# A decoder layer on one Trainium2 core: the third norm's sum of squares, one weight block's remainder, the first loads and the final norm's root, each placed otherwise

## The chip, the cores and the metric

The kernel runs on one core of a Trainium2 chip. The metric is the device time of one execution in microseconds (us). The core has a matmul engine (TensorE, PE), three engines for elementwise work (VectorE or DVE, ScalarE or ACT, GpSimd or POOL), a queue for transfers (SyncE, SP), and sixteen DMA engines. Each engine works through its own list of instructions in order; semaphores hold an instruction until what it needs is there.

## The reference, cut to what matters

One layer for 256 tokens of width 1024, in float32:

```python
h = rmsnorm(x, norm_mix_g)
proj = h @ w_in                               # q, k, v, gu, gv, two gates
y_a = moba_attention(rope(q), rope(k), v) @ moba_w_proj
y_b = gmlp_spatial_gating(gu, gv, ...) @ gmlp_w_proj
x = x + (sigmoid(gate_a) * y_a + sigmoid(gate_b) * y_b) @ w_out
x = x + cross_attention(rmsnorm(x, norm_xa_g), rmsnorm(mem, norm_mem_g), ...)
h = rmsnorm(x, norm_ffn_g)                    # the third norm
q = h @ peer_w_q                              # 8 heads, 2 halves of 128
s1, i1 = top_k(q[half 0] @ subkeys[0].T, 16); s2, i2 = top_k(q[half 1] @ subkeys[1].T, 16)
e, g = best 16 of the sums s1 + s2, softmax   # 16 of 128*128 experts for each head
x = x + sum over e of g * gelu(h . w_down[e]) * w_up[e]
return rmsnorm(x, final_g)
# rmsnorm(x, g) = x * rsqrt(mean(x*x) + 1e-6) * g
```

The last sum is computed densely: all 16384 experts are multiplied, 128 blocks of the down product and 128 blocks of the up product, with weights that are zero for the experts not chosen.

## The kernel before

**Number format.** PE gets each float32 matrix as two parts, a rounded one and the remainder. A weight block (128 x 1024, 512 KB) is loaded into a tile `raw` by SP's queue, ACT casts it to `hi` (L140), and another engine subtracts, `lw = raw - hi` (L142). A product then takes three matmuls: hi by hi, lo by hi, hi by lo (L179 to L181 in `mm3`). Activations are split in the same way by `split` (L170, L173, L175).

**Order.** The order of work is written out by hand. `stream` lists the weight blocks: 84 of the front part (`f`), then those of the down (`d`) and up (`u`) products. `take(kind)` hands out the next block, and at the same time issues the cast and remainder of the block two further on (`conv_to`, LEAD = 2) and loads up to four further still (`load_to`, four `raw` tiles), and then the postponed pieces in `later`. So when block m is used, block m+2 is being converted.

**Who makes the remainder.** `lo_engine` chooses: VectorE for front blocks below 70, POOL from 70 on and for the first five `d` blocks, VectorE after that. Blocks in the list `spread` (52 to 59, 65 to 69) have their remainder put off: two half-width subtractions on VectorE go into the list `half`, and `half.pop(0)()` at a later place in the code issues one of them (L146).

**Cross-attention.** For head h, `xquery(h)` computes queries, `xscore(h)` the scores, their row maximum (L629, L630) and the exponentials on ACT (L632); `xscale(h)` divides by the sum (L652, L654); `xtrans` transposes (L641) and copies (L644, L646). Two `nm_.step()` calls (blocks 62 and 63) finish the values `vm` from the memory, which are scaled at L688 and L689; `xvalue` (L661) multiplies. The first `nm_.step()` stands ahead of `xscore(3)`, and it converts block 64, whole, before the change.

**Third norm.** `Squares.add` squares one of eight pieces of x on ACT (L261) and adds it to a running sum on VectorE (L267), so there are seven adds. `Squares.matmul` sums over partitions on PE (L273). The 16 blocks 68 to 83 of `peer_w_q` run in a loop over n; each calls `take`, multiplies (`tblock`), copies the result on ACT, and runs `pscore(n-1)`: two score matmuls (L752), a copy on ACT (L753) and a top-16 pass on VectorE (`best`, L728 to L736). The products use unnormalised activations; the root `r3` (`newton`: ACT's root and five small VectorE instructions) is needed only for the later normalised activations `h3`, which `norm_block(k)` makes one piece at a time. `bcast` spreads the root over the partitions by a matmul (L286). Before the change the squares are added for pieces 0 to 2, 3 to 5, and 6 and 7 at n = 0, 1, 2; the sum's matmul stands in the middle of block n = 3; the broadcast stands at n = 7, and the eight norm blocks at n = 7 to 14.

**After the loop.** VectorE selects the 16 best pairs of each head and looks up their indices, in pieces between which the first 22 `down` blocks are placed.

**End.** `ulast` runs the last two up blocks for token half t = 0, then t = 1. For each t, ACT squares both halves of the row (L1082), with their sums; VectorE adds these and forms the mean (L1084, L197), ACT takes the root (L1086), VectorE multiplies by the gain (L1087), refines the root and scales (L1095; POOL for t = 0), and the result is stored.

Of the kernel before, what the change touches and what calls it, by code (L numbers as in the profile page):

```python
# [16 lines left out]
F32 = mybir.dt.float32  # L17
# [4 lines left out]
AF = mybir.ActivationFunctionType  # L22
OP = mybir.AluOpType
# [3 lines left out]
D = 1024  # L27
S = 256
KD = 8
EPS = 1e-6  # L30
# [15 lines left out]
N_XO, N_PQ = 4, 16  # L46
# [43 lines left out]
def body(tc, I, out, dbg=None):  # L90
# [3 lines left out]
    V, A, P, T, SY = nc.vector, nc.scalar, nc.gpsimd, nc.tensor, nc.sync  # L94
# [10 lines left out]
    nf = I["wf"].shape[0]  # L105
    steps = plan()
    stream = [("f", n) for n in range(nf)] + [x for x in steps if x[0] in "du"]
    raws, convs, later = {}, {}, []
    spread, half = [*range(52, 60), nf - N_PQ - 3, *range(nf - N_PQ - 2, nf - N_PQ + 2)], []
    pos = {"load": 0, "conv": 0, "take": 0}  # L110

    def load_to(n):
        while pos["load"] < min(n, len(stream)):
            m = pos["load"]
            kind, idx = stream[m]
            raw = wst.tile([128, 1024], F32, name="raw", bufs=RAW)
            SY.dma_start(raw, {"f": I["wf"], "d": I["wd"], "u": I["wu"]}[kind][idx])
            raws[m] = raw
            pos["load"] += 1

    def lo_engine(m):
        kind, idx = stream[m]
        if kind == "f":
            return V if idx < nf - N_PQ + 2 else P
        if kind == "d" and idx < FIRST:
            return P
        return V
# [23 lines left out]
    def take(kind):  # L151
        m = pos["take"]
        assert stream[m][0] == kind
        pos["take"] += 1
        conv_to(m + 1 + LEAD)
        load_to(m + 1 + LEAD + RAW)
        for fn in later:
            fn()
        later.clear()
        return convs.pop(m)  # L160


    def sl(k):
        return (slice(None), k, slice(None))

    def tsl(t):
        return slice(t * 128, (t + 1) * 128)

    def split(hi, lo, src, scale=1.0, eng=None):
        A.activation(hi, src, AF.Copy, scale=scale)  # L170
        e = eng or V
        if isinstance(scale, float) and scale == 1.0:
            e.tensor_sub(lo, src, hi.bitcast(F32))  # L173
        else:
            e.scalar_tensor_tensor(lo, src, scale, hi.bitcast(F32), op0=OP.mult, op1=OP.subtract)  # L175

    def mm3(ps, w, wsl, x, xsl, start, stop):
        (wh, wl), (xh, xl) = w, x
        T.matmul(ps, wh[wsl], xh[xsl], start=start, stop=False)  # L179
        T.matmul(ps, wh[wsl], xl[xsl], start=False, stop=False)  # L180
        T.matmul(ps, wl[wsl], xh[xsl], start=False, stop=stop)  # L181
# [14 lines left out]
    def mean_sq(v, ms, width):  # L196
        V.tensor_scalar(v, ms, 1.0 / width, EPS, op0=OP.mult, op1=OP.add)  # L197
# [5 lines left out]
    mid = ctx.enter_context(tc.tile_pool(name="mid", bufs=1))  # L203
# [4 lines left out]
    def pair(name, pool, n=KD, w=S):  # L208
        return (pool.tile([128, n, w], F32R, name=name + "h"), pool.tile([128, n, w], F32R, name=name + "l"))
# [4 lines left out]
    def pmm():  # L214
        return pf.tile([128, S], F32, name="mm", bufs=3)

    def pat(shape):
        return pf.tile(shape, F32, name="at", bufs=3)
# [4 lines left out]
    xT = fo.tile([128, KD, S], F32, name="xT")  # L223
# [5 lines left out]
    raw0 = wst.tile([128, 1024], F32, name="raw", bufs=RAW)  # L229
    raws[0] = raw0  # L230
    pos["load"] = 1
    for k in range(2):
        SY.dma_start(raw0[:, k * 512:(k + 1) * 512], I["wf"][0][:, k * 512:(k + 1) * 512])
        SY.dma_start(xT[:, k], I["xT"][:, k])
    for j in range(1, 4):
        SY.dma_start(xT[:, 2 * j:2 * j + 2], I["xT"][:, 2 * j:2 * j + 2])
        load_to(j + 1)
    warm = cst.tile([128, 1], F32, name="warm")
    A.activation(warm, ones, AF.Sqrt)
    wps = pat([128, 128])  # L240
# [48 lines left out]
    def tblock(w, x, n=KD, base=0, mid=None):  # L289
        ps = pmm()  # L290
        for k in range(n):
            if mid and k == n // 2:
                mid()
            c = (base + k) * 128
            mm3(ps, w, (slice(None), slice(c, c + 128)), x, sl(k), k == 0, k == n - 1)
        return ps
# [23 lines left out]
    raw0 = raws.pop(0)  # L320
# [57 lines left out]
    for c in range(4):  # L378
        for nm in ("q", "k"):
            first = c == 0  # L380
            ps = tblock(take("f"), xg, mid=(sqp.matmul if nm == "q" else rope_norm) if first else None)
# [139 lines left out]
    for c in range(4):  # L521
        ps = tblock(take("f"), xg)
# [37 lines left out]
    for c in range(4):  # L560
        ps = tblock(take("f"), mg)
# [42 lines left out]
    pq = Squares(fp2, "x1")  # L604
    for c in range(KD):
        ps = tblock(take("f"), mp)
# [30 lines left out]
    def xtrans(t, h):  # L637
        ps = pat([128, 2, 2, 128])
        for i in range(2):
            for sb in range(2):  # L640
                T.transpose(ps[:, i, sb], Px[t][:, h + i, sb * 128:(sb + 1) * 128], ident)  # L641
        PT = fp2.tile([128, 2, 2, 128], F32, name="PT", bufs=4)
        if t:
            V.tensor_copy(PT, ps)  # L644
        else:
            A.copy(PT, ps)  # L646
        XT_[t, h] = PT


    def xscale(h):  # L650
        xr = fp2.tile([128, 2], F32, name="xr", bufs=4)
        V.reciprocal(xr, xs[:, :, 2, h])  # L652
        for t in range(2):
            V.tensor_scalar(Px[t][:, h], Px[t][:, h], xr[:, t:t + 1], None, op0=OP.mult)  # L654
# [26 lines left out]
    xscale(2)  # L681
    xtrans(0, 0)
    xtrans(1, 0)
    skh = [fo.tile([128, 8, 128], F32, name="kT")]
    P.dma_start(skh[0], I["skT"][:, 0:8])
    xscale(3)
    nm_.step()
    V.tensor_scalar(vm[:, 0], nm_.ps[0], rm[:, 0:1], None, op0=OP.mult)  # L688
    A.activation(vm[:, 1], nm_.ps[1], AF.Copy, scale=rm[:, 1:2])  # L689
# [8 lines left out]
    xg2 = pair("xg", fo)  # L698
    rp = rs1.enter_context(tc.tile_pool(name="route", bufs=2, side="right", reuse_waits="tile"))
    S1 = rp.tile([128, 8, 2, 2, 128], F32, name="S1", bufs=1)  # L700
    x2T = rp.tile([128, KD, S], F32, name="x2T", bufs=1)
    pq = Squares(fp2, "x2")
    for c2 in range(4):
        w = take("f")
        for c in range(2):
            cc = 2 * c2 + c
            ps = tblock(w, oxT, n=4, base=4 * c)
# [32 lines left out]
    def norm_block(k):  # L740
        hx = fp2.tile([128, S], F32, name="hx", bufs=3)
        V.scalar_tensor_tensor(hx, x2T[:, k], gcol[:, 3, k:k + 1], r3bc, op0=OP.mult, op1=OP.mult)
        later.append(lambda: split(h3[0][:, k], h3[1][:, k], hx))
# [12 lines left out]
    for n in range(16):  # L756
        sk = skh[n // 8][:, n % 8]
        w = take("f")
        if n == 4:
            v3 = fp2.tile([128, 2], F32, name="v3")  # L760
            sq_sum(pq, v3)
        if n == 5:
            r3 = newton(fp2, v3, 2, "r3")
            V.tensor_copy(r3c, r3)
        ps = tblock(w, xg2, mid=pq.matmul if n == 3 else None)
        qp = fp2.tile([128, S], F32, name="qp", bufs=2)
        A.copy(qp, ps)
        qps[n] = (qp, sk)
        if n < 3:
            for k in range(3 * n, min(3 * n + 3, 8)):  # L770
                pq.add(x2T[:, k], A, V)
        if n == 7:
            bcast(r3, r3bc)
            norm_block(0)
        if 8 <= n < 15:
            norm_block(n - 7)
        if n > 0:
            pscore(n - 1)
    pscore(15)
# [6 lines left out]
    gp = g.enter_context(tc.tile_pool(name="exp", bufs=2, reuse_waits="tile"))  # L786
    pp = g.enter_context(tc.tile_pool(name="pexp", bufs=1, space=PSUM, reuse_waits="tile"))
    yps = [[pp.tile([128, 512], F32, name=f"y{t}{z}") for z in range(2)] for t in range(2)]
# [89 lines left out]
    n, spent = 0, 0.0  # L878
# [39 lines left out]
    for j in range(3):  # L918
        ps = mblock()[:, :S]
# [112 lines left out]
    for n, x in enumerate(rest):  # L1032
# [16 lines left out]
        else:  # L1049
            up_a(x[1])  # L1050
            up_b(x[1])
            w = take("u")
# [18 lines left out]
    sqs = wst.tile([128, D], F32, name="raw", bufs=RAW)  # L1071
    for t in range(2):
        ulast(ws, [UP[i2] for i2 in range(128 - TAILN, 128)], t)
        scale = P.tensor_scalar if t == 0 else V.tensor_scalar
        fs = gp.tile([128, 2], F32, name="fs")
        yg = wst.tile([128, D], F32, name="raw", bufs=RAW)
        fm = gp.tile([128, 1], F32, name="fm")
        fv = gp.tile([128, 1], F32, name="fv")
        sq = gp.tile([128, 1], F32, name="fsq")
        for z in range(2):  # L1080
            zs = slice(z * 512, (z + 1) * 512)
            A.activation(sqs[:, zs], yps[t][z], AF.Square, accum_out=fs[:, z:z + 1])  # L1082
            if z == 1:
                V.tensor_add(fm, fs[:, 0:1], fs[:, 1:2])  # L1084
                mean_sq(fv, fm, D)
                A.activation(sq, fv, AF.Sqrt)  # L1086
            V.tensor_mul(yg[:, zs], yps[t][z], fg[:, zs])  # L1087
        fy = gp.tile([128, 1], F32, name="fy")
        V.reciprocal(fy, sq)
        fu = gp.tile([128, 1], F32, name="fu")  # L1090
        V.scalar_tensor_tensor(fu, fy, fy, fv, op0=OP.mult, op1=OP.mult)
        V.tensor_scalar(fu, fu, -0.5, 1.5, op0=OP.mult, op1=OP.add)
        for z in range(2):
            zs = slice(z * 512, (z + 1) * 512)
            scale(yg[:, zs], yg[:, zs], fy, fu, op0=OP.mult, op1=OP.mult)  # L1095
            (SY if z == 0 or t == 0 else A).dma_start(out[0, tsl(t), zs], yg[:, zs])
    g.close()
    ctx.close()

# [73 lines left out]
```

## Time and profile before

| | |
|---|---|
| median of three runs | 1051.2 us |
| lowest, highest | 1049.24, 1052.67 us |
| the profiled execution | 1049.31 us, of which the span shown is 1047.6 us |
| PE busy | 1029.6 us, 98% of the span |
| VectorE busy | 763.3 us, 73% |
| ACT busy | 593.9 us, 57% |
| POOL busy | 63.5 us, 6% |
| mean granted clock of PE | 0.996 of full speed |

The lines of the timeline have the start and the duration in us, the engine, the source line, the operation, the tile written and the tiles read, the shape and a count. In brackets stands for how long the engine was idle before it, and what ended that. The lines of a window have busy us and the number of instructions for PE, PE's weight loads, DVE, ACT and POOL, then PE's granted clock, the share of the DMA engines and GB/s. Lines of the waits have the total in us, how often, and the longest.

### The profile page before, as it was taken

Reading aid. Unit: us, or ns where it says so; the run is one execution under the profiler, and the core shown is the slowest. Engines: PE = TensorE matmul, PEld = TensorE weight load, DVE = VectorE, ACT = ScalarE, POOL = GpSimd, SP = SyncE. Lnnn points to the kernel's source line nnn. Section 1 sums busy time; section 2 is a strip of 40 time slices with the busy share of each in tenths; the row PEclk is TensorE's granted clock in tenths of the full one; section 3 lists DMA queues with packets and bytes.
Section 4 is the critical chain, followed back from the end, with each engine's and each line's share of the span. In section 5 each row is a group of like instructions: output and inputs, shape, how many; then the busy total and the mean of one; then the engine's idle time right before and its main releaser. Section 6 shows DMA issues by size and latency. Waiting matters only on the chain.

```text
span 1047.6 us, 19742 instructions
## 1 busy us (share of the span) xinstructions
PE 1029.6 (98%) x7862; PEld 953.1 (91%) x7862; DVE 763.3 (73%) x1502; ACT 593.9 (57%) x935; POOL 63.5 (6%) x53
## 2 busy tenths in 40 slices
PE   9999999998999999999999999999999999999997
PEld 7989999998999999999988998899999988888885
DVE  6765797688999899965656565666799766666666
ACT  6955745665654567755454545454678654444554
POOL 0400000016740000000000000000000000000000
PEclk9999999999999999999999999999999999999999
DMA  8644655554456534456666566656444565656562
GB/s 291 232 138 133 197 173 168 174 164 140 157 165 203 171 118 155 147 180 189 194 188 194 185 198 187 195 185 198 149 157 140 181 192 191 196 188 197 187 198 101
DMA packets 52365, 185.84 MB, mean 177 GB/s; under 512 B 5937, under 2 KB 6833, under 8 KB 52145
## 3 DMA queue, kind: packets, MB, share of 16 engines
q1 hardware_dynamic: 51552, 183.20, 54.6%
q8 instruction: 61, 1.00, 0.4%
q0 software_dynamic: 288, 1.05, 0.3%
q10 hardware_dynamic: 432, 0.34, 0.1%
q14 instruction: 32, 0.25, 0.1%
HBM read 183.52 MB, written 1.05 MB: 176 GB/s over the span
## 4 chain that ended last, share of the span: by engine, by line
PE 89%; DVE 7%; ACT 2%; DMA 1%; issue 1%; DVEq 0%; SPq 0%; ACTq 0%
PE A L179 11%; PE y L1016 11%; PE y L1013 11%; PE y L1012 11%; PE A L181 11%; PE A L180 11%; PE mm L179 5%; PE mm L180 5%; PE mm L181 5%; PE m L985 2%; PE m L984 2%; DVE lw L142 1%; ACT hi L140 1%; DMA raw<-in_wf 1%; PE at L406 1%; PE nat L312 1%
## 5 line engine op out<-in xcount | busy, mean ns | idle before, releaser
L142 DVE TENSOR_TENSOR lw<-raw,hi 128x1024 fp32r<-128x1024 f32 (+1 forms) x309 | 377.1, 1222 | 229.9 <-ACT hi L140 229.0
L140 ACT CAST hi<-raw 128x1024 fp32r<-128x1024 f32 (+1 forms) x341 | 355.4, 1043 | 189.4 <-issue 139.5
L179 PE MATMUL A<-mgh,hi 128*128 128x256 f32 x1024 | 290.2, 283 | 0.0
L181 PE MATMUL A<-mgh,lw 128*128 128x256 f32 x1024 | 287.6, 281 | 1.8 <-DVE lw L142 1.8
L180 PE MATMUL A<-mgl,hi 128*128 128x256 f32 x1024 | 287.4, 281 | 0.0
L181 PEld LDWEIGHTS A<-mgh,lw 128*128 128x128 f32 x1024 | 195.8, 191 | 2.2 <-DVE lw L142 2.2
L1012 PE MATMUL y<-hi,gahl 128*128 128x512 f32 x504 | 196.1, 389 | 0.0
L1013 PE MATMUL y<-lw,gahl 128*128 128x512 f32 x504 | 196.1, 389 | 0.0
L180 PEld LDWEIGHTS A<-mgl,hi 128*128 128x128 f32 x1024 | 192.8, 188 | 2.2
L179 PEld LDWEIGHTS A<-mgh,hi 128*128 128x128 f32 x1024 | 192.3, 188 | 2.2
L1016 PE MATMUL y<-hi,gahl 128*128 128x512 f32 x504 | 155.2, 389 | 0.0
L800 ACT ACTIVATE aring<-A 128x256 f32<-128x256 f32 x128 | 49.2, 384 | 161.7 <-PE A L181 161.7
L179 PE MATMUL mm<-xgh,hi 128*128 128x256 f32 x416 | 119.1, 286 | 0.3 <-DVE q L368 0.3
L181 PE MATMUL mm<-xgh,lw 128*128 128x256 f32 x416 | 116.4, 280 | 0.0
L180 PE MATMUL mm<-xgl,hi 128*128 128x256 f32 x416 | 116.4, 280 | 0.0
L1016 PEld LDWEIGHTS y<-hi,gahl 128*128 128x128 f32 x504 | 94.6, 188 | 19.6
L1012 PEld LDWEIGHTS y<-hi,gahl 128*128 128x128 f32 x504 | 94.6, 188 | 17.4
L1013 PEld LDWEIGHTS y<-lw,gahl 128*128 128x128 f32 x504 | 94.6, 188 | 17.4
L179 PEld LDWEIGHTS mm<-xgh,hi 128*128 128x128 f32 x416 | 79.0, 190 | 1.3 <-issue 0.7
L181 PEld LDWEIGHTS mm<-xgh,lw 128*128 128x128 f32 x416 | 79.1, 190 | 0.0
L180 PEld LDWEIGHTS mm<-xgl,hi 128*128 128x128 f32 x416 | 78.9, 190 | 0.1
L986 ACT ACTIVATE G<-m 128x512 f32<-128x512 f32 x64 | 66.0, 1141 | 5.0 <-PE m L985 2.3
(272 smaller groups left out, 1246.8 us busy)
## 6 DMA issues: line engine op xcount, KB each, us to landing
raw<-in_wd SPq DMA_DIRECT2D x128, 512.0 KB, 3.8
raw<-in_wu SPq DMA_DIRECT2D x128, 512.0 KB, 4.1
raw<-in_wf SPq DMA_DIRECT2D x83, 512.0 KB, 3.7
memT<-in_memT SPq DMA_DIRECT2D x1, 1024.0 KB, 7.3
xT<-in_xT SPq DMA_DIRECT2D x3, 256.0 KB, 6.7
out_y<-raw SPq DMA_DIRECT2D x3, 256.0 KB, 2.0
raw<-in_wf SPq DMA_DIRECT2D x2, 256.0 KB, 3.5
wmT<-in_wsT SPq DMA_DIRECT2D x1, 512.0 KB, 6.2
```

The costliest lines, as they stand in the source:

```text
L140: A.copy(hi[:, ps], raw[:, ps])
L142: lo_engine(m).tensor_sub(lw[:, ps], raw[:, ps], hi[:, ps].bitcast(F32))
L179: T.matmul(ps, wh[wsl], xh[xsl], start=start, stop=False)
L180: T.matmul(ps, wh[wsl], xl[xsl], start=False, stop=False)
L181: T.matmul(ps, wl[wsl], xh[xsl], start=False, stop=stop)
L800: A.activation(a, ps, AF.Gelu_apprx_tanh)
L984: T.matmul(ps[:, t], a1[at], bh[at], start=True, stop=False)
L985: T.matmul(ps[:, t], a1[at], bl[at], start=False, stop=True)
L986: A.activation(Gq[q][:, :, s * TG + c:s * TG + c + 8].rearrange("p i t -> p t i"), ps, AF.Copy, scale=1.0 / 16384.0)
L1012: T.matmul(yps[t][z], gh[:, tsl(t)], wh[:, zs], start=False, stop=False, skip_group_check=True)
L1013: T.matmul(yps[t][z], gh[:, tsl(t)], wl[:, zs], start=False, stop=False, skip_group_check=True)
L1016: T.matmul(yps[t][z], gl[:, tsl(t)], wh[:, zs], start=False, stop=False, skip_group_check=True)
```

## The change

Four edits:

1. Third norm. The remainders of blocks 70 and 71 move from POOL to VectorE. The squares go 4, 3, 1 over n = 0, 1, 2. The sum's matmul moves from the middle of block n = 3 to its end, behind ACT's copy of the result in the order of the code and ahead of `pscore(2)`. The root's broadcast and the norm blocks move one block earlier, to n = 6 and n = 6 to 13.
2. Cross-attention. The remainder of block 64 is put off in two halves; one is issued behind the first two transposes, the other behind `xscale(3)`.
3. First loads. `xT` comes in three transfers (two, two and four of its eight pieces) instead of five (one, one, two, two, two), ordered with the first weight blocks as the diff shows.
4. Final norm. ACT squares with a scale of 1/32, so that its sums are already means; eps is added to the first half's sum while the second is still being computed, and ACT takes the root of the second sum with that as its bias. For t = 1 the two small factors are multiplied first, and the row is scaled half by ACT and half by VectorE.

```diff
-    spread, half = [*range(52, 60), nf - N_PQ - 3, *range(nf - N_PQ - 2, nf - N_PQ + 2)], []
+    spread, half = [*range(52, 60), nf - N_PQ - 4, nf - N_PQ - 3, *range(nf - N_PQ - 2, nf - N_PQ + 2)], []
...
-            return V if idx < nf - N_PQ + 2 else P
+            return V if idx < nf - N_PQ + 4 else P
...
-    for k in range(2):
-        SY.dma_start(raw0[:, k * 512:(k + 1) * 512], I["wf"][0][:, k * 512:(k + 1) * 512])
-        SY.dma_start(xT[:, k], I["xT"][:, k])
-    for j in range(1, 4):
-        SY.dma_start(xT[:, 2 * j:2 * j + 2], I["xT"][:, 2 * j:2 * j + 2])
-        load_to(j + 1)
+    SY.dma_start(raw0[:, 0:512], I["wf"][0][:, 0:512])
+    SY.dma_start(xT[:, 0:2], I["xT"][:, 0:2])
+    SY.dma_start(raw0[:, 512:1024], I["wf"][0][:, 512:1024])
+    SY.dma_start(xT[:, 2:4], I["xT"][:, 2:4])
+    load_to(2)
+    SY.dma_start(xT[:, 4:8], I["xT"][:, 4:8])
+    load_to(4)
...
     xtrans(1, 0)
+    half.pop(0)()
...
     xscale(3)
+    half.pop(0)()
     nm_.step()
...
-        ps = tblock(w, xg2, mid=pq.matmul if n == 3 else None)
+        ps = tblock(w, xg2)
...
-        if n < 3:
-            for k in range(3 * n, min(3 * n + 3, 8)):
-                pq.add(x2T[:, k], A, V)
-        if n == 7:
+        for k in ((0, 1, 2, 3), (4, 5, 6), (7,))[n] if n < 3 else ():
+            pq.add(x2T[:, k], A, V)
+        if n == 3:
+            pq.matmul()
+        if n == 6:
             bcast(r3, r3bc)
-            norm_block(0)
-        if 8 <= n < 15:
-            norm_block(n - 7)
+        if 6 <= n < 14:
+            norm_block(n - 6)
...
-            A.activation(sqs[:, zs], yps[t][z], AF.Square, accum_out=fs[:, z:z + 1])
-            if z == 1:
-                V.tensor_add(fm, fs[:, 0:1], fs[:, 1:2])
-                mean_sq(fv, fm, D)
-                A.activation(sq, fv, AF.Sqrt)
+            A.activation(sqs[:, zs], yps[t][z], AF.Square, scale=1.0 / 32.0, accum_out=fs[:, z:z + 1])
+            if z == 0:
+                V.tensor_scalar(f0, fs[:, 0:1], EPS, None, op0=OP.add)
+            else:
+                A.activation(sq, fs[:, 1:2], AF.Sqrt, bias=f0)
             V.tensor_mul(yg[:, zs], yps[t][z], fg[:, zs])
+        V.tensor_scalar(fv, fs[:, 1:2], f0, None, op0=OP.add)
...
-        for z in range(2):
-            zs = slice(z * 512, (z + 1) * 512)
-            scale(yg[:, zs], yg[:, zs], fy, fu, op0=OP.mult, op1=OP.mult)
-            (SY if z == 0 or t == 0 else A).dma_start(out[0, tsl(t), zs], yg[:, zs])
+        if t == 0:
+            for z in range(2):
+                zs = slice(z * 512, (z + 1) * 512)
+                P.tensor_scalar(yg[:, zs], yg[:, zs], fy, fu, op0=OP.mult, op1=OP.mult)
+                SY.dma_start(out[0, tsl(t), zs], yg[:, zs])
+        else:
+            fr = gp.tile([128, 1], F32, name="fr")
+            V.tensor_scalar(fr, fu, fy, None, op0=OP.mult)
+            A.activation(yg[:, 0:512], yg[:, 0:512], AF.Copy, scale=fr)
+            V.tensor_scalar(yg[:, 512:], yg[:, 512:], fr, None, op0=OP.mult)
+            SY.dma_start(out[0, tsl(t), 512:], yg[:, 512:])
+            A.dma_start(out[0, tsl(t), 0:512], yg[:, 0:512])
```

More of the change, by code (lines that the diff above doesn't have):

```diff
@@ L1073, in body @@
         ulast(ws, [UP[i2] for i2 in range(128 - TAILN, 128)], t)
-        scale = P.tensor_scalar if t == 0 else V.tensor_scalar
         fs = gp.tile([128, 2], F32, name="fs")
         yg = wst.tile([128, D], F32, name="raw", bufs=RAW)
-        fm = gp.tile([128, 1], F32, name="fm")
+        f0 = gp.tile([128, 1], F32, name="fm")
         fv = gp.tile([128, 1], F32, name="fv")
```

## The prediction, made before the change was timed

> **What bounds the kernel now.** I read the page first, then what TensorE (PE) waited for, then the timeline around each of its waits.
>
> ```profile
> span 1047.6 us, 19742 instructions
> PE 1029.6 (98%) x7862; PEld 953.1 (91%) x7862; DVE 763.3 (73%) x1502; ACT 593.9 (57%) x935; POOL 63.5 (6%) x53
> ```
>
> PE is busy in all but 18 us. So an edit pays only where it takes away a PE wait, a stretch in which PE runs slowly, or time at either end of the span. The longest waits of PE, in the columns total, times, longest:
>
> ```profile
> PE at L273 <- DVE sq L267: 4.2, 1, 4.2
> PE A L181 <- DVE lw L142: 1.8, 2, 1.4
> PE nat L312 <- ACT hi L140: 1.2, 1, 1.2
> ```
>
> The first is the third norm's and the third the start's, both touched here. The change also works on a gap in cross-attention and on the final norm, which lies behind PE's last matmul.
>
> **Third norm.** PE around its wait (start, duration in us), and a window with its granted clock (the column PEclk, third from the end):
>
> ```profile
> 238.53 0.61 PE L752 MATMUL at<-kT,qp 128*128 128x128 f32 x4
> 238.89 0.36 PE L179 MATMUL mm<-xgh,hi 128*128 128x256 f32 x1
> ...
> 240.27 0.28 PE L181 MATMUL mm<-xgh,lw 128*128 128x256 f32 x1
> 244.70 0.81 PE L273 MATMUL at<-ones,sq 128*128 128x1 f32 x4 [4.15 <-DVE sq L267]
> ...
> 248.58 0.36 PE L179 MATMUL mm<-xgh,hi 128*128 128x256 f32 x1
> ```
> ```profile
> 245.00:246.00 1.00, 1.00 (x6) 1.00 (x6) 1.00 (x9) 0.00 (x0) 0.00 (x0) 0.50 0.83 319
> ```
>
> In the middle of block n=3, PE idles 4.15 us for the sum of squares, and then runs the other half of the block at half clock. Why the sum is late, on POOL and on VectorE (DVE):
>
> ```profile
> 232.62 4.93 POOL L142 TENSOR_TENSOR lw<-raw,hi 128x1024 fp32r<-128x1024 f32 x2 [12.57 <-ACT hi L140]
> 238.04 2.59 POOL L142 TENSOR_TENSOR lw<-raw,hi 128x1024 fp32r<-128x1024 f32 x1 [0.48 <-ACT hi L140]
> ```
> ```profile
> 233.75 7.70 DVE L267 TENSOR_TENSOR sq<-sq 128x256 f32<-128x256 f32 x5 [1.62 <-ACT sq L261]
> ...
> 243.71 0.94 DVE L267 TENSOR_TENSOR sq<-sq 128x256 f32<-128x256 f32 x2
> ```
>
> The last two adds take 0.47 us each. The five ahead of them, beside POOL's remainders of blocks 70 to 72, take 7.70: an add seems to wait until POOL's instruction ends. Between the fifth and the last two lies a whole top-16 pass, 241.45 to 243.71, some 2.3 us.
>
> The Trainium skill says why (SBUF — State Buffer, "Who interferes with whom"): a VectorE instruction with two SBUF inputs and a GpSimd instruction that reads SBUF exclude each other for a whole instruction, and issue order decides who waits. The trace agrees, 7.70 us against 5 x 0.47. By that rule VectorE's new remainders could block, or be blocked, as well; their place in time decides.
>
> *What the edit does.* The remainders of blocks 70 and 71 go from POOL (4.93 us for both) to VectorE, at 1.23 us each (the 128x1024 row under cross-attention below). POOL starts with block 72 at 238.04. The seven adds go 3, 3, 1 over n=0, 1, 2 instead of 2, 3, 2; the sum's matmul moves from the middle to the end of block 3, ahead of its scores.
>
> ```profile
> 231.51 1.03 ACT L140 CAST hi<-raw 128x1024 fp32r<-128x1024 f32 x1
> ...
> 232.98 1.04 ACT L261 ACTIVATE sq<-x2T 128x256 f32<-128x256 f32 x3
> 233.92 1.04 ACT L140 CAST hi<-raw 128x1024 fp32r<-128x1024 f32 x1
> ...
> 236.66 0.36 ACT L753 COPY S<-at 128x256 f32<-128x256 f32 x1
> ```
>
> VectorE step by step, in the old clock. The remainder of block 70 runs 232.55 to 233.8, behind ACT's cast. Four squares, at a third of 1.04 each, are ready by 234.4; three adds end by 235.2. That fourth square puts ACT's cast for block 71 to 234.3 to 235.3; the remainder follows to 236.6, over 2 us before block 3 begins. Squares 4 to 6 lie ahead of ACT's score copy at 236.66, as before; three adds end at 238.0. The pass of n=0 takes 2.3, to 240.3. The last add finds POOL in block 72, until 238.04 + 2.59 = 240.63, and ends at 241.1. No other add meets POOL.
>
> PE: the first half of block 3 took 238.89 to 240.39 (240.27 + 0.12), the second would take 1.4 at the same pace, to 241.8. The sum is ready 0.7 us earlier: no wait. The sum's matmul (0.81 at half clock, so 0.4) and the scores (0.36, 238.53 to 238.89) put block 4 at 242.6 instead of 248.58: **6.0** us gained. Both effects are in it, the 4.15 of waiting and 1.9 of slow matmuls.
>
> *What is late next.* VectorE may hold PE back further on:
>
> ```profile
> 265.00:300.00 35.00, 34.93 (x299) 34.74 (x298) 34.93 (x166) 21.54 (x39) 26.40 (x14) 1.00 0.49 158
> ```
> ```profile
> 303.91 0.39 PE L181 MATMUL A<-mgh,lw 128*128 128x256 f32 x1 [0.39 <-DVE lw L142]
> ```
>
> From 265 to 300 VectorE (third pair of numbers) is as full as PE, and at 303.91 PE waits for it. So PE keeps the 6.0 only if VectorE comes as much earlier there. I take it that it does: the adds fall from 7.70 + 0.94 to 3.7 us (seven at 0.47, plus 0.4 of waiting) against 2.46 for the two remainders, 2.5 less; the rest of VectorE's work in these blocks is released by PE's scores, which come 6.0 earlier, and after the stall it idled for them. The norm blocks and the broadcast of the root, one block earlier, are the same instructions in another place; they use that idle time and leave less behind block 15.
>
> Lower end 3: the last add misses its gap and waits out block 73 too (2.6 more, less the 0.7 of slack, and some slow clock). Upper end 7.8, if VectorE gains more than PE and both its L142 waits close (1.8).
>
> **Cross-attention: one block's remainder in halves.**
>
> ```profile
> 212.06 0.57 ACT L632 ACTIVATE Px<-at,xs,r2s 128x256 f32<-128x256 f32 x1 [2.15 <-DVE xr L652]
> ```
> ```profile
> 209.94 1.23 DVE L142 TENSOR_TENSOR lw<-raw,hi 128x1024 fp32r<-128x1024 f32 x1 [1.54 <-ACT hi L140]
> 211.09 0.69 DVE L629 TENSOR_REDUCE xs<-at 128x2 f32<-128x512 f32 x1
> ```
> ```profile
> 213.32 0.44 PE L641 MATMUL at<-ident,Px 128*128 128x128 f32 x2 [0.87 <-DVE PT L644]
> 213.91 0.88 PE L641 MATMUL at<-ident,Px 128*128 128x128 f32 x6 [0.15 <-DVE Px L654]
> 214.83 4.11 PE L661 MATMUL mm<-PT,vm 128*128 128x128 f32 x32
> ```
>
> VectorE idles 1.54 us for ACT's cast, runs the remainder (1.23), and only then the row maximum of the last head, on which its exponentials, scaling, transposes and values hang. Now the maximum runs ahead of the cast, and ACT's exponentials start as the cast ends, near 209.9 instead of 212.06. PE's gaps of 0.87 and 0.15 close. One half stands ahead of the scaling of `vm`, but the chain into it starts 2.1 us earlier, so the value product should start about 1.2 earlier than 214.83. Term: **1.2**; ends 0 (the value product waits for the halves instead of the transposes) and 1.5.
>
> **First loads.**
>
> ```profile
> 9.46 1.14 ACT L140 CAST hi<-raw 128x512 fp32r<-128x512 f32 x2 [0.40 <-DMA raw<-in_wf]
> ```
> ```profile
> 6.00:7.00 1.00, 1.00 (x6) 0.72 (x4) 0.41 (x1) 0.97 (x2) 0.00 (x0) 1.00 0.93 217
> 11.00:12.00 1.00, 1.00 (x5) 0.81 (x6) 1.00 (x3) 0.66 (x3) 0.00 (x0) 1.00 1.08 438
> ```
>
> PE's 1.2 us wait ends with block 1's cast, which waits for its load. The bytes ahead of that load stay the same; two pieces of 128 KB become part of one of 256 KB. The DMA engines are about equally busy at 217 GB/s, among the small pieces, and at 438, among whole blocks, so I expect that load up to 0.4 us earlier. Against it, the first matmul needs 128 KB more, and block 2 stands behind 256 KB more of `xT`, 0.6 us at 438 GB/s. SP's queue has two issues fewer. Term: **0.2**, from -0.6 to 0.7.
>
> **Final norm.** The path behind the last matmul, for t=1:
>
> ```profile
> 1041.18 0.19 ACT L1082 ACTIVATION_READ_ACCUMULATOR raw<-y 128x1 f32 x1
> 1042.10 0.20 ACT L1086 ACTIVATE fsq<-fv 128x1 f32<-128x1 f32 x1 [0.72 <-DVE fv L197]
> 1044.25 0.35 ACTq L1096 DMA_DIRECT2D out_y<-raw  x1
> ```
> ```profile
> 1043.21 1.00 DVE L1095 TENSOR_SCALAR raw<-raw,fy,fu 128x512 f32<-128x512 f32 x2
> ```
>
> The root no longer waits for VectorE: it can stand at 1041.4, 0.7 earlier, and the gain product now runs beside the square instead of between sum and reciprocal. One more small product costs 0.2, so the scaling starts 0.5 earlier. Its two halves, 1.00 in series, run on ACT and VectorE together, which saves another 0.3. Term: **0.8**, from 0.2 to 1.2.
>
> **Sum.** 6.0 + 1.2 + 0.2 + 0.8 = 8.2 us. The profiled execution took 1049.31 us, so it would take 1041.1. The median of the runs, 1051.2, stands 1.9 above it; against that, 1043.0.
>
> **Rivals.**
> - *The last add misses its gap* between POOL's blocks 72 and 73, for which it is 0.3 us early. Then PE waits some 1.9 us at the end of block 3, and the third norm brings 3: gain 5.2, 1046.0. Issue order, in the rule named above, would do it if POOL's next instruction is let in first. For it: the margin is small. Against it: five adds did get through in 7.70 us beside POOL's back-to-back remainders.
> - *VectorE sets the end of the routing.* PE comes early but waits at L181 near 303.91, because VectorE has gained only its 2.5: 2.5 + 2.2 from the other three, 1046.5. Against it: VectorE idled for PE after the stall.
> - *Slower: the broadcast of the root stalls PE.* It moves to the end of block 6 and needs the third root:
>
> ```profile
> 256.47 0.17 DVE L764 COPY r3c<-r3r 128x2 f32<-128x2 f32 x1
> ```
>
>   PE comes for it three blocks after 242.6, at 3.3 us each, about 252.3. If the root stayed put at 256.6, PE would wait 4.3 us and run slowly again, which eats the 6.0; each top-16 pass more ahead of it adds 2.3. It decides from a root later than about 259; with two passes more, 1053. Against it: the sum is done 3.5 us earlier than before, and the root follows two passes behind it.
> - *The sum is late anyway*, held by ACT's squares instead of the adds, and PE waits at the end of block 3 as it did in the middle: only the small terms stay, 2.2: 1049.0.
>
> **How the numbers follow.** The forecast has 0.70, the missed gap 0.12, VectorE's bound 0.08, the sum late anyway 0.06, the broadcast 0.04. About 0.3% (3.2 us) can be told from no change here. The first three are faster by more, the fourth is within it, the broadcast half within and half slower: 0.90, 0.08, 0.02; I move 0.02 to slower, for a cause that I have not seen. The forecast's own range, with most terms near their values, is 1040 to 1045.5. To hold 8 in 10 with the two weaker gains it reaches to 1047, and down to 1038.5, where the profiled execution's own time is the base and VectorE's waits close.
>
> **What would show it.** Right: no PE wait at L273 and PEclk 1.00 through block 3; adds of under 0.5 except one; the last head's row maximum ahead of its remainder; ACT's last root directly behind its accumulator read; PE's two L181 waits no longer than before. Wrong: a second add of over 2 us, a PE wait at L286, an L181 wait of several us, or a first matmul that starts much later.

## The result, and the profile after

The changed kernel takes 1042.38 us (median of four runs, 1041.45 to 1042.81) against 1051.11: a ratio of 0.9916, 95% interval 0.9899 to 0.9934, so 8.8 us less (6.9 to 10.6). The forecast was 1043.0. The profiled execution took 1042.34 us, 7.0 less than the profiled one of before, where the sum gave 1041.1 against that execution's own time. Why the two differ is, in part, below.

The page and PE's waits (total, times, longest):

```profile
span 1040.6 us, 19734 instructions
PE 1026.7 (99%) x7862; PEld 951.5 (91%) x7862; DVE 760.2 (73%) x1505; ACT 594.4 (57%) x936; POOL 58.1 (6%) x51
```
```profile
PE A L181 <- DVE lw L142: 3.1, 2, 2.8
PE nat L313 <- ACT xgh L170: 1.9, 1, 1.9
PE at L243 <- DVE ones L226: 1.0, 1, 1.0
```

The third norm's wait is gone, and so is the one in cross-attention for VectorE's copy (0.87 us at L641 before). At the start PE now waits 1.9 us for its first activations (`xgh`), where it waited 1.2 us for block 1's cast, and the waits at L181 come to 3.1 us instead of 1.8.

**Third norm.** VectorE, POOL and PE from the timeline after (start, duration in us):

```profile
232.50 1.49 DVE L268 TENSOR_TENSOR sq<-sq 128x256 f32<-128x256 f32 x3
234.05 1.23 DVE L142 TENSOR_TENSOR lw<-raw,hi 128x1024 fp32r<-128x1024 f32 x1
235.19 1.48 DVE L268 TENSOR_TENSOR sq<-sq 128x256 f32<-128x256 f32 x3
...
238.94 0.52 DVE L268 TENSOR_TENSOR sq<-sq 128x256 f32<-128x256 f32 x1
```
```profile
236.79 2.39 POOL L142 TENSOR_TENSOR lw<-raw,hi 128x1024 fp32r<-128x1024 f32 x1 [17.98 <-ACT hi L140]
239.44 2.38 POOL L142 TENSOR_TENSOR lw<-raw,hi 128x1024 fp32r<-128x1024 f32 x1 [0.27 <-ACT hi L140]
```
```profile
240.54 0.50 PE L274 MATMUL at<-ones,sq 128*128 128x1 f32 x4
240.91 0.69 PE L755 MATMUL at<-kT,qp 128*128 128x128 f32 x4
```

The seven adds take 3.5 us instead of 8.64. Only the last meets POOL, just at the end of block 72: it ends 0.28 us behind POOL's remainder and 1.1 us before PE asks for the sum. Block 3's scores start at 240.91 instead of 248.08.

**Where the rest went.** PE at the end of the routing and its clock there (PEclk, third from the end):

```profile
351.49 0.38 PE L181 MATMUL A<-mgh,lw 128*128 128x256 f32 x1 [2.75 <-DVE lw L142]
```
```profile
351.00:352.00 1.00, 0.51 (x4) 0.51 (x5) 1.00 (x2) 0.00 (x0) 0.00 (x0) 1.00 0.00 0
352.00:353.00 1.00, 1.00 (x7) 1.00 (x7) 1.00 (x2) 0.00 (x0) 0.00 (x0) 0.53 0.62 127
```

A wait of 2.75 us, and half clock behind it for some 3 us (PEclk 0.50 from 353 to 355, 0.77 in the microsecond after). The profile of before had 1.44 us here and full clock:

```profile
359.33 0.38 PE L181 MATMUL A<-mgh,lw 128*128 128x256 f32 x1 [1.44 <-DVE lw L142]
```
```profile
360.00:361.00 1.00, 1.00 (x11) 1.00 (x10) 1.00 (x2) 0.00 (x0) 0.00 (x0) 1.00 0.65 131
```

**The final norm** of t=1:

```profile
1034.19 0.60 ACT L1084 ACTIVATE raw<-y 128x512 f32<-128x512 f32 x1 [0.67 <-PE y L1028]
1034.69 0.19 ACT L1084 ACTIVATION_READ_ACCUMULATOR raw<-y 128x1 f32 x1
1034.91 0.29 ACT L1088 ACTIVATE fsq<-fs,fm 128x1 f32<-128x1 f32 x1
1034.91 0.69 DVE L1089 TENSOR_TENSOR raw<-y,raw 128x512 f32<-128x512 f32 x1 [0.61 <-ACT raw L1084]
...
1037.28 0.35 ACTq L1107 DMA_DIRECT2D out_y<-raw  x1
```

From ACT's square to its store's issue it takes 3.09 us instead of 3.56. The root stands right behind the accumulator read. The gain product does not run beside the square: it waits for ACT, as it did before.

### The profile page after: what moved, and what is told of

Read it like the earlier page. It is cut to its first block, busy times and chain, and to the rows that moved or that the text cites. A ratio compares the mean times of both kernels' runs of the same rounds, so it can differ in the third digit from the quotient of the medians.

```text
span 1040.6 us, 19734 instructions
## 1 busy us (share of the span) xinstructions
PE 1026.7 (99%) x7862; PEld 951.5 (91%) x7862; DVE 760.2 (73%) x1505; ACT 594.4 (57%) x936; POOL 58.1 (6%) x51
## 4 chain that ended last, share of the span: by engine, by line
PE 89%; DVE 8%; ACT 1%; DMA 1%; issue 1%; DVEq 0%; ACTq 0%
PE y L1016 11%; PE y L1019 11%; PE y L1015 11%; PE A L179 10%; PE A L181 9%; PE A L180 9%; PE mm L179 6%; PE mm L180 6%; PE mm L181 6%; DVE lw L142 3%; PE m L988 2%; PE m L987 2%; DVE jk L850 1%; DMA raw<-in_wf 1%; DVE acc L840 1%; PE nat L313 1%
## 5 line engine op out<-in xcount | busy, mean ns | idle before, releaser
L181 PE MATMUL A<-mgh,lw 128*128 128x256 f32 x1024 | 287.5, 281 | 3.1 <-DVE lw L142 3.1
L181 PEld LDWEIGHTS A<-mgh,lw 128*128 128x128 f32 x1024 | 195.9, 191 | 3.5 <-DVE lw L142 3.5
L181 PE MATMUL mm<-xgh,lw 128*128 128x256 f32 x416 | 116.0, 279 | 0.0
L181 PEld LDWEIGHTS mm<-xgh,lw 128*128 128x128 f32 x416 | 78.6, 189 | 0.0
```

## The experiments

**Each edit alone**, on the kernel before, all four on one chip beside it (1050.87 us).

*The third norm alone.*
```diff
-            return V if idx < nf - N_PQ + 2 else P
+            return V if idx < nf - N_PQ + 4 else P
# and the adds 4, 3, 1; pq.matmul() behind block 3; bcast at n == 6; norm_block(n - 6)
```


> The kernel before with the first edit alone (third norm). Theory: the sum of squares was late because VectorE's adds could not run beside POOL's remainders; with the two remainders on VectorE, PE's 4.15 us wait at L273 and the half clock behind it are gone, block 4 starts 5.9 to 6.0 us earlier, and of that 4.5 to 6 us reach the end, since VectorE's routing work holds some back at PE's last L181 wait (1.44 us before, longer now): about 1046. Rival, VectorE sets the end of the routing: only its 2.5 us of saved work reach the end, PE's last L181 wait grows by 3 us or more: 1048.7.

1043.49 us, ratio 0.9931 (0.9919 to 0.9944): 7.3 us faster (5.9 to 8.5), more than the 4.5 to 6 expected. Nearly the whole change. In its trace PE does not wait at L273, and block 3's scores start at 242.06 instead of 248.08. The rival's 1048.7 is out. PE's last L181 wait is 2.74 us in its profile, as in the changed kernel, but without half clock behind it; that profile is of the fastest of its five runs.

*Cross-attention alone.*
```diff
-    spread, half = [*range(52, 60), nf - N_PQ - 3, ...
+    spread, half = [*range(52, 60), nf - N_PQ - 4, nf - N_PQ - 3, ...
# and half.pop(0)() behind xtrans(1, 0) and behind xscale(3)
```


> The kernel before with the second edit alone (cross-attention, block 64's remainder in halves). Theory: the row maximum of the last head comes ahead of the remainder, the value product starts 1.2 to 1.9 us earlier and all of it reaches the end, since nothing behind it is fuller than PE: 1049.2 to 1050. Rival: the value product waits for the halves, or the gain is eaten by a longer L181 wait at the end of the routing: 1051.

1048.75 us, 0.9981 (0.9973 to 0.9990): 2.0 us faster (1.1 to 2.8). The value product starts at 212.69; before, at 214.83, of which 0.5 is the start of the program (PE's last score product stands at 206.30 instead of 206.78). So 1.7 us there, and 1.9 at the end of the value products (3.84 us instead of 4.11); by the time none of it is lost. The rival is out. The row maximum (L629) now stands ahead of the remainder's halves (L146):

```profile
207.84 0.69 DVE L629 TENSOR_REDUCE xs<-at 128x2 f32<-128x512 f32 x1
...
209.96 0.69 DVE L146 TENSOR_TENSOR lw<-raw,hi 128x512 fp32r<-128x512 f32 x1
...
211.29 0.68 DVE L146 TENSOR_TENSOR lw<-raw,hi 128x512 fp32r<-128x512 f32 x1
```
```profile
212.69 3.84 PE L661 MATMUL mm<-PT,vm 128*128 128x128 f32 x32
```

*First loads alone.*
```diff
+    SY.dma_start(xT[:, 0:2], ...); ...; SY.dma_start(xT[:, 2:4], ...); load_to(2)
+    SY.dma_start(xT[:, 4:8], ...); load_to(4)
```


> The kernel before with the third edit alone (first loads). Theory from the trace of the changed kernel: PE's first product waits for 256 KB of xT instead of 128 KB, starts 1.4 us later after an idle time of about 2 us, runs some 3 us at half clock, and block 1's cast comes 0.6 us later: 0.6 us slower at cross-attention, about 1051.7. Rival, the prediction's: the wider transfers are faster and the load of block 1 comes no later: 0.2 us faster, 1050.9, with the late first product hidden by the wait for block 1.

1051.25 us, 1.0004 (0.9991 to 1.0017): the times do not tell, either side stays open by them. Block 1's cast supports the theory: it starts at 9.85, against 9.46 in the kernel before. In the eight profiles with the old loads it starts between 8.91 and 9.67 (mean 9.31), in the six with the wider ones between 9.71 and 10.09 (mean 9.94), so the wider loads bring it about 0.6 us later. The last score product of cross-attention is no measure for that: it stands at 207.21 here and at 206.78 before, but with the old loads it varies from 205.52 to 206.78 and with the wider ones from 206.73 to 208.97. The first real product starts at 6.54 instead of 5.33, behind 1.0 us of idle time, and the half clock that was expected behind it did not come. How much of the 0.6 us reaches the end is not shown.

*The final norm alone.*
```diff
+            A.activation(sqs[:, zs], yps[t][z], AF.Square, scale=1.0 / 32.0, accum_out=fs[:, z:z + 1])
+                A.activation(sq, fs[:, 1:2], AF.Sqrt, bias=f0)
# and for t == 1 the two halves on ACT and VectorE
```


> The kernel before with the fourth edit alone (final norm). Theory from the trace of the changed kernel: from ACT's last square to its store's issue 3.1 us instead of 3.56, so 0.5 us: 1050.6. Rival, the prediction's 0.8: 1050.3; it would need the gain product to run beside the square, not behind its accumulator read.

1050.08 us, 0.9992 (0.9983 to 1.0001): 0.8 us faster (none to 1.8). In its trace 3.08 us lie between square and store issue, 0.5 less than before. The times can't part the two numbers, the trace can: 0.5. The four edits alone add to 9.7 us, the whole change brought 8.8 (6.9 to 10.6): no interaction is shown.

**What in the third norm does it: who subtracts, or the order.** Two kernels, each with one half of that edit on the kernel before (1050.69 us beside them).

*The two remainders on VectorE, order as before.*
```diff
-            return V if idx < nf - N_PQ + 2 else P
+            return V if idx < nf - N_PQ + 4 else P
```


> The kernel before with only the two remainders moved to VectorE; adds (2, 3, 2), the sum's matmul in the middle of block 3 and the norm blocks stay. Theory, the adds were held by POOL's remainders: five adds now take 2 to 2.5 us instead of 7.70, the two last still stand behind a top-16 pass and under block 72, so the sum is ready near 241.4 in the old clock and PE still waits 0.9 us at L273, without half clock behind it: about 5 us faster than before, 1046 (if the last add also waits out block 73: PE waits 3.3 us, 1049). Rival, the places of adds and matmul were the cause: little change, 1050.5.

1046.41 us, 0.9952 (0.9937 to 0.9968): 5.0 us faster (3.4 to 6.6), as the theory had it. VectorE's adds and PE's wait in its timeline:

```profile
234.90 1.48 DVE L267 TENSOR_TENSOR sq<-sq 128x256 f32<-128x256 f32 x3
...
238.65 1.33 DVE L267 TENSOR_TENSOR sq<-sq 128x256 f32<-128x256 f32 x2
```
```profile
240.03 0.61 PE L273 MATMUL at<-ones,sq 128*128 128x1 f32 x4 [0.76 <-DVE sq L267]
```

0.76 us of waiting (0.9 expected), and no half clock. This profile is of the fastest of the seven runs, 1042.19 us, 4.2 under their median. Five of the seven lie at 1045.82 and above, with a mean granted clock of 0.997 or 0.998 instead of 0.999. Half clock in some stretch, such as behind PE's last L181 wait, where this profile has none, would fit them; it is not shown.

*The new order, remainders on POOL as before.*
```diff
+        for k in ((0, 1, 2, 3), (4, 5, 6), (7,))[n] if n < 3 else ():
+            pq.add(x2T[:, k], A, V)
+        if n == 3:
+            pq.matmul()
# and bcast at n == 6, norm_block(n - 6)
```


> The kernel before with only the new order of the third norm (adds 3, 3, 1, matmul at the end of block 3, norm blocks one earlier); POOL keeps the remainders of blocks 70 and 71. Theory, the adds are held by POOL's remainders: only one or two adds get through at each end of a POOL instruction, so six adds ahead of the first top-16 pass end no earlier than 241 to 244, the sum comes near or behind 244, PE waits 2 to 5 us at the end of block 3 and falls to half clock: 1049 to 1052. Rival, the places were the cause: no wait at L273, about 6 us faster, 1045.

1051.18 us, 1.0008 (0.9998 to 1.0019): no gain. Its timeline:

```profile
233.37 10.66 DVE L267 TENSOR_TENSOR sq<-sq 128x256 f32<-128x256 f32 x6 [1.62 <-ACT sq L261]
246.29 0.41 DVE L267 TENSOR_TENSOR sq<-sq 128x256 f32<-128x256 f32 x1
```
```profile
232.25 2.41 POOL L142 TENSOR_TENSOR lw<-raw,hi 128x1024 fp32r<-128x1024 f32 x1 [12.57 <-ACT hi L140]
234.97 2.40 POOL L142 TENSOR_TENSOR lw<-raw,hi 128x1024 fp32r<-128x1024 f32 x1 [0.31 <-DVE sq L267]
237.67 2.39 POOL L142 TENSOR_TENSOR lw<-raw,hi 128x1024 fp32r<-128x1024 f32 x1 [0.30 <-ACT hi L140]
240.33 2.36 POOL L142 TENSOR_TENSOR lw<-raw,hi 128x1024 fp32r<-128x1024 f32 x1 [0.27 <-ACT hi L140]
```
```profile
246.76 1.01 PE L273 MATMUL at<-ones,sq 128*128 128x1 f32 x4 [5.17 <-DVE sq L267]
```

Six adds in 10.66 us, and PE waits 5.17. Taken one by one, the first four adds end at 234.95, 237.65, 240.34 and 242.97, each 0.28 or 0.29 us behind the end of one of POOL's remainders: one add gets through for each. POOL does not wait for the adds here. The bracket of its second remainder names VectorE's add, but ACT's cast of that block ends at 234.89, 0.08 us ahead of POOL's start, as the casts of the next two blocks do. In the kernel before, the three remainders that started while an add ran (blocks 71 to 73) took 2.52 to 2.59 us; here they take 2.36 to 2.41. So the engine is the cause. The order alone is worth nothing; with the engine changed it takes away the last 0.76 us of waiting. By time the whole edit brought 7.3 us and the engine alone 5.0, on different chips; how much of the 2.3 between them is the order's is not shown.

**The end of the routing.** The remainder that PE waits for at its last L181 wait stands on VectorE behind the routing's last instructions, a stretch in which VectorE makes no remainder. `D0` down blocks are placed among the routing's pieces and `D1` behind them.

```diff
-D0, D1 = 22, 4
+D0, D1 = 23, 3
```


> The changed kernel with 23 down blocks placed between the routing's pieces and 3 behind them, instead of 22 and 4: the remainder of block 24 comes ahead of the routing's last instructions. Theory, what is left of the third norm's gain is lost at PE's wait for that remainder (2.75 us) and the half clock behind it (1.6): the wait moves to the next block and shrinks to about 1.2 us, with no half clock, so some 3 us faster than the changed kernel, 1039.5. Rival, VectorE is the bound as a whole: the remainder put ahead delays the routing's end by 1.2 us and PE waits as long at the transposes or the next remainder: 1042.4 or more.

1039.66 us, 0.9896 of the kernel before (0.9879 to 0.9914), where the changed kernel has 0.9916: about 2 us of the 3 expected. PE's last L181 wait in its profile:

```profile
353.59 0.38 PE L181 MATMUL A<-mgh,lw 128*128 128x256 f32 x1 [1.38 <-DVE lw L142]
357.18 0.44 PE L924 MATMUL m<-ident,R 128*128 128x128 f32 x2 [0.30 <-DVE i1T L926]
```

1.38 us (1.2 expected), and no half clock behind it: the mean granted clock of this profile is 0.999, of the changed kernel's 0.996.

```diff
-D0, D1 = 22, 4
+D0, D1 = 24, 2
```


> The changed kernel with 24 and 2. Theory as for 23 and 3: both remainders come ahead of the routing's end, PE no longer waits at L181 there, and reaches the transposes near 355.7, by when the routing is done (352.7): up to 4 us faster than the changed kernel, 1038.5. Rival, VectorE as the bound: the routing's end comes 2.5 us later, PE waits at the transposes instead: 1042.4 or more.

1040.63 us, 0.9905 (0.9888 to 0.9922). No L181 wait there, but 1.55 us at the transposes, which the rival named. Of the up to 4 us expected, 1 to 2 came by the ratio and the median, and the interval holds the changed kernel's 0.9916. From 23 and 3 it is not told apart. One block more is enough.

**The changed kernel again, and three more on the same chip** (before: 1050.67 us).

> The changed kernel as it is, beside the next three on one chip: 1042.4, faster than before by 8.4 us.

1042.05 us, 0.9912 (0.9896 to 0.9928), 9.2 us less; runs from 1040.01 to 1045.76.

*With the old first loads* (the third edit taken back).


> The changed kernel with the first loads of the kernel before. Theory, the wider first loads cost 0.4 to 0.7 us: 1041.9, with block 1's cast near 9.5 us instead of 10.1. Rival, the start is hidden or the wider loads pay: 1042.4 or more.

1041.77 us, 0.9908 (0.9893 to 0.9923). Against 1042.05 the times do not tell. ACT's cast of block 1 in this kernel, and then in the changed kernel (its first profile):

```profile
9.12 1.14 ACT L140 CAST hi<-raw 128x512 fp32r<-128x512 f32 x2 [0.53 <-DMA raw<-in_wf]
```
```profile
10.08 1.14 ACT L140 CAST hi<-raw 128x512 fp32r<-128x512 f32 x2 [0.35 <-DMA raw<-in_wf]
```

*With old loads and 23 and 3.*


> The changed kernel with the first loads of the kernel before and with 23 and 3 down blocks instead of 22 and 4. Theory, the two gains add: 0.5 us for the loads and 2.7 for the routing's end, 1039.2. Rival, the loads' gain is lost at PE's remaining wait of 1.4 us at L181: 1039.7.

1039.17 us, 0.9887 of before (0.9872 to 0.9903), 11.9 us less: the lowest ratio of all, though its interval overlaps that of 23 and 3 with the wide loads. It is the changed kernel without its third edit and with one down block more among the routing's pieces. Against the kernel above, which has the same loads and 22 and 4, the one number brings 2.6 us, and the runs do not overlap (1038.36 to 1039.68 against 1039.86 to 1043.22). That the loads' part adds is not shown by the times (1039.66 with 23 and 3 and the wide loads).

*With more warming products.*
```diff
-WARM = 10
+WARM = 16
```


> The changed kernel with 16 warming products at the start instead of 10, so that PE has no idle time ahead of its first real product and no half clock behind it. Theory, the start is set by the load of block 1 and not by PE: no change, 1042.4. Rival, the late first product and the half clock (up to 1.5 us) reach the end: 1041.4.

1041.35 us, 0.9909 (0.9892 to 0.9925): not told apart from 1042.05 by time. In its trace PE has no idle time ahead of its first product. PE's first product with block 1's remainder stands at 11.10, 1.39 us behind the start of block 1's cast (9.71). In the changed kernel, with 1.92 us of idle time and PEclk 0.50 from 8 to 10 us, it stands at 11.52, 1.44 us behind that cast (10.08). So the start follows the load of block 1; the late first product and the half clock behind it cost 0.05 us there.

## Why the prediction was right, and where its steps were off

*Third norm.* 6.0 us were predicted up to block 4. Between the scores of n=0 and block 3's the trace gives 5.9: those of n=0 moved by 1.25 us (235.25 to 234.00, cross-attention less the start), those of block 3 by 7.17. The path was as worked out: three adds, remainder, three adds, top-16 pass, one add at the end of POOL's block 72. Alone, the edit gave 7.3 us, with an interval that holds 6.0. The Trainium skill's rule that it rested on (SBUF — State Buffer, "Who interferes with whom": two SBUF inputs against a GpSimd read, one waits for the whole instruction) was borne out on VectorE's side, with 10.66 us for six adds. On POOL's side only 0.1 to 0.2 us show, in the remainders that began while an add ran.

*What is late next.* The step "PE keeps the 6.0 only if VectorE comes as much earlier there" held at 303.91: the same wait, 0.39 us, now stands at 296.77, 7.14 earlier. Behind it, the forecast "PE's two L181 waits no longer than before" failed in the profile (2.75 against 1.44), but the change did not make it longer. In the kernels with one other edit alone (cross-attention, loads, final norm), which still have the wait at L273, that wait is 2.73 us too. With cross-attention alone:

```profile
357.24 0.58 PE L181 MATMUL A<-mgh,lw 128*128 128x256 f32 x1 [2.73 <-DVE lw L142]
```

The profile of before was the exception. From the first L181 wait to the second, its PE took 2.83 us for each down block, from one ACT activation to the next; all other profiles but that of 24 and 2 blocks have 2.72 there. With PE slower, it reached VectorE's late remainder later, waited less, and did not fall to half clock. That execution, at 1049.31, was 1.9 us under the median. So one half of the rival "VectorE sets the end of the routing" was true all along, in nearly every profile: PE waits there for VectorE, and that cost both kernels the same. Its other half, that VectorE gains only 2.5 us, was not: at the first L181 wait, which VectorE's remainder ends, it had gained 7.14.

*Base.* The sum fits the medians (8.2 against 8.7 measured) better than the profiled execution (7.0), whose base had less of this wait and none of the half clock. That is about half of the reason. From the first L181 wait to the transposes the profile of before took 61.66 us, the changed kernel 62.60, and the four other kernels that keep the long wait at L273 62.49 to 62.58: 0.9 of the 1.9 us by which that execution lay under the median. The rest is not traced. Taking the median as the base was right, without the reason being known. Part of the fit is luck: by the traces the terms of the loads and the final norm were 1.1 us too high together and that of cross-attention 0.5 too low.

*Cross-attention*: 1.2 predicted, 1.7 at the value product and 2.0 (1.1 to 2.8) in time. The term was too small: the value product started 0.5 us earlier than worked out, and the value products also took 3.84 us instead of 4.11; why they did was not tried.

*First loads*: +0.2 predicted, about -0.6 measured by the cast of block 1 (9.46 to 10.08, and 0.6 between the means of all profiles with either loads). The step that failed is "I expect that load up to 0.4 us earlier": the rate of 217 GB/s in one window was taken as a property of the small pieces. From 6 to 7 us the wide version does move more (301 GB/s), but from 4 to 5 us it moves less, and the load does not come forward. The kernel before and the changed kernel there:

```profile
4.00:5.00 1.00, 1.00 (x7) 1.00 (x7) 0.69 (x1) 0.46 (x2) 0.00 (x0) 1.00 0.91 229
```
```profile
4.00:5.00 1.00, 0.86 (x8) 0.66 (x6) 0.66 (x1) 0.31 (x1) 0.00 (x0) 1.00 0.77 139
```

The six profiles with the wider loads have 103 to 157 GB/s in this window, the eight others 225 to 264. What sets that dip, and whether it alone delays the load, was not tried. A sign that the prediction had named for being wrong, a first matmul that starts much later, showed too: 6.78 instead of 5.33.

*Final norm*: 0.8 predicted, 0.5 measured. The step that failed is "the gain product now runs beside the square". The gain product starts only behind ACT's square of the same `y` and its accumulator read, and so the reciprocal at 1035.64 stands 1.45 us behind the square's start; it was 1.89 before. With one small product more, the scaling starts 0.2 us earlier instead of 0.5; its two halves save the 0.3 that was expected. What keeps the gain product behind ACT was not tried.

## What to carry to other kernels

When small VectorE instructions take several times their usual duration, look at what POOL does in the same window: here moving two 2.4 us instructions off POOL was worth 5 us, and reordering without that nothing. A profiled execution is one draw: where the median is 0.2% off its time, look for a wait that other runs have and it has not, before the gain is counted from its rows. And where an engine lags behind PE in a long stretch, look at which of its outputs PE needs next and whether a block of other work stands ahead of it; one number in the plan was worth 2.6 us here.

## What the runs showed that was not expected

PE's pace differed between runs of the same instructions: 2.72 or 2.83 us for each down block, constant from one PE wait to the next, at full granted clock both times. What switches it was not found. And half clock does not follow a wait of a given length. Of the ten profiles with a wait of 2.72 to 2.75 us at L181, eight show PEclk 0.50 behind it. Two ran on at full clock, the third norm alone (2.74) and the two remainders alone (2.72): 6.2 us from the wait's end to the next wait at the transposes, where the changed kernel took 7.9. Each of these two profiles is of the fastest run of its kernel. At the start of the changed kernel 1.92 us of idle time were enough for half clock.
